# Two context weight pairs in one pass beside the first norm, and FFN token differences from whole normed values, made factor by factor

## The chip, the cores and the metric

One core of one Trainium2 chip runs the whole program. The metric is device microseconds from the first to the last instruction of one execution, as a median of several runs. TensorE (PE in the rows) multiplies, VectorE (DVE) and ScalarE (ACT) work on elements, GpSimd (POOL) takes some of the elementwise work, SyncE (SP) starts the transfers between main memory and the on-chip memory. Every engine takes its own instructions strictly in the order in which the built program lists them; semaphores hold an instruction until what it needs is there.

## The reference

One layer over 1024 latent tokens and 256 context tokens of width 1024, in fp32. What the change touches is this:

```python
hc = modulate(rms_norm(ctx, norm1_gain[layer]), csh1, csc1)
feats_c, post_c = mixer_inputs(hc, w_in[layer], ...)      # keys and values of the context, two mixers of 4 heads
hx = modulate(rms_norm(x, norm1_gain[layer]), sh1, sc1)   # first norm of the 1024 tokens
...
x = x + g1 * mixer_output(...)                            # ends in the product with w_out
x = x + g2 * swiglu(modulate(rms_norm(x, norm2_gain[layer]), sh2, sc2), w_ffn_in[layer], w_ffn_out[layer])
```

`modulate(h, shift, scale)` is `h * (1 + scale) + shift`, and `swiglu` is `(silu(gate) * up) @ w_ffn_out` with 2816 hidden channels.

## The kernel before

Features lie on the 128 partitions and tokens along the free axis, in two halves of 512 tokens. Each fp32 operand of a product is held as two parts: `split` (L190 to L192) writes the high part with a ScalarE cast (L191) and the low part with a VectorE subtraction (L192), and a product is three matmuls, high by high, high by low and low by high. A weight tile of 128x512 is loaded by SyncE into one of four tiles named `raw`, and split into one of seven tiles named `fw`. A scheduler places the instructions of all engines in an order that it works out when the program is built; the order of the Python lines is its priority.

**Context and first norm (L439 to L545).** The context's keys and values need four weight pairs, (pair, kt) with eight tiles of 128 features each; `ctx_tiles(pair, kts)` (L453) issues six matmuls for a tile, `ctx_load` (L445) loads and splits the next tile in the order of `ctx_order`. Pairs 0 and 1 run together while the modulation vectors are made. Then, in L530 to L534, each tile of pair 2 stands beside `scaled_x(0, kt)`, which multiplies a tile of the first token half by its root mean square (L484, VectorE), scales and shifts it twice on ScalarE (L402 for the high part, L404 for the whole value) and subtracts (L407, VectorE). Pair 3 follows in L536 to L541 after the sums of squares of the second half, with the loads of the first projection's weights (`plain_pair`) among it. Behind it come the gate products (L638) and the first keys, values, queries and gates (L265, in L644 to L656).

**Out-projection, second norm and the FFN's first blocks (L1131 to L1280).** For each token half, the out-projection gives `xf[hf]`, eight tiles, and two tiles `acc` of summed squares. `norm_steps` (L1142) then multiplies by the root mean square (L1152, VectorE) and calls `modulate_split` (L400): high part on ScalarE (L402), the whole value on GpSimd (L406, in place in `xf`), low part on VectorE (L407). `px0`, which holds `xf[0]`, is closed after the norm (L1183), so of the first half only the two parts remain, named `A` in the rows.

The FFN makes its first gate block and first up block in plain form, `plain_half` (L267), once for each token half. From the second block on it uses a seven-product form (`winograd_block`, L276), which needs differences of the token tiles: x11 and x21 are the upper and lower feature halves of the first tokens, x12 and x22 those of the second tokens. `right_factors(k)` (L1207) makes them for one k, with the first half put together again from its two parts:

```python
        tt(d, x22, x12, ALU.subtract)
        split(t3[0][k], t3[1][k], d)
        tt(x12, x12, b11[0][k].bitcast(F32), ALU.subtract)
        tt(x12, x12, b11[1][k].bitcast(F32), ALU.subtract)
        split(t1[0][k], t1[1][k], x12)
```

and so on to `t2` and to the value whose split in L1269 is `t4`. The weights of a seven-product block come from `Factors.make` (L234): s1 = a21 + a22 and s2 = s1 - a11 on VectorE, a11 - a21 on GpSimd, a12 - s2 on VectorE (all L237), each split. A block gives TensorE seven products of twelve matmuls in the tiles `ch` and `ts`; between them ScalarE copies the running `ch` tile into a tile `u` (L299), and TensorE may add the next product to `ch` only then. `run_blocks` puts the next block's first product after the fifth of the present one.

**The hidden tiles.** Of the plain blocks, ScalarE copies the result (L1255), and GpSimd multiplies up by the silu of gate (`up_done`, L1201). The four results of the first block are kept in `held_back`, and SyncE stores them (L1236) ahead of later loads. In SyncE's queue they stand before four loads of `cp` tiles for the kernel's last stage (L1378), and before the `raw` tiles of the second seven-product block.

## Time and profile before

| | us |
|---|---|
| median of 3 runs (1636.03, 1641.23, 5503.55) | 1641.23 |
| the profiled execution, its own time | 1639.88 |
| its span, first to last instruction | 1638.1 |
| TensorE busy in the span | 1571.9 (96%) |
| VectorE busy | 999.9 (61%) |
| ScalarE busy | 740.6 (45%) |
| GpSimd busy | 427.2 (26%) |
| mean granted TensorE clock, of full speed | 0.989 |

TensorE is busy nearly throughout, so a change that leaves the matmuls as they are can only move the rest: stretches in which TensorE stands still, and stretches after them in which its matmuls start further apart. In the waits view a row names who waited and which instruction released it. In the timeline a row is one or several like instructions with their start and duration, and behind them in brackets the idle time before and its releaser. Matmuls overlap, so the spacing of their starts is what one costs.

### The profile page before, as it was taken

The page shows a single profiled execution, that of the slowest core. Times are in us where ns is not written, and L with a number is a line of the kernel's source. Part 1 is how long each engine was busy: PE and PEld are TensorE (multiplying, and loading weights), DVE is VectorE, ACT ScalarE, POOL GpSimd, SP SyncE. Part 2 cuts the span into 40 slices and gives each one's busy share as a digit, 9 for nine tenths or more (in the row PEclk, how much of TensorE's full clock was granted, in tenths as well). Part 3 has the DMA queues.
Part 4 walks back from the last instruction along what each step waited for, and adds up shares of the span by engine and source line. Part 5 has one row for each costly group of instructions (what it writes and reads, how often), then busy time and mean ns, then how long its engine had stood idle before and what let it go on. Part 6 is the DMA issues. An engine that isn't in the chain of part 4 may idle for free.

```text
span 1638.1 us, 22335 instructions
## 1 busy us (share of the span) xinstructions
PE 1571.9 (96%) x7478; PEld 1282.6 (78%) x7478; DVE 999.9 (61%) x1843; ACT 740.6 (45%) x1430; POOL 427.2 (26%) x444
## 2 busy tenths in 40 slices
PE   7999979899999999999999998999999999999997
PEld 2678767778888777888888876888888888887887
DVE  4677787657657777766445786555555555546343
ACT  4676544444544575665223453334433334533230
POOL 0003225443335445420220254222222221001001
PEclk9999989999999999999999999999999999999998
DMA  8753547666666666647456413223222324835531
GB/s 293 265 156 105 154 141 241 193 197 198 185 180 222 200 207 206 189 143 263 142 167 198 130 45 103 78 84 96 91 90 77 95 86 148 271 102 181 167 96 52
DMA packets 178291, 255.47 MB, mean 156 GB/s; under 512 B 18128, under 2 KB 75984, under 8 KB 178176
## 3 DMA queue, kind: packets, MB, share of 16 engines
q1 hardware_dynamic: 176304, 251.95, 49.3%
q10 hardware_dynamic: 1872, 2.10, 0.4%
q8 instruction: 59, 0.97, 0.2%
q14 instruction: 56, 0.46, 0.1%
HBM read 197.60 MB, written 56.38 MB: 155 GB/s over the span
## 4 chain that ended last, share of the span: by engine, by line
PE 63%; DVE 8%; DMA 6%; issue 4%; ACT 3%; POOL 3%; SPq 0%; DVEq 0%; POOLq 0%; ACTq 0%
PE ch L265 20%; PE ts L265 15%; PE ch L1345 2%; PE ch L1344 2%; PE ch L1343 2%; PE ts L1343 2%; PE ts L1345 2%; PE ts L1344 2%; DMA stg<-wada 2%; PE ch L113 1%; PE ts L113 1%; PE ch L111 1%; PE ts L112 1%; PE ch L112 1%; PE ts L111 1%
## 5 line engine op out<-in xcount | busy, mean ns | idle before, releaser
L192 DVE TENSOR_TENSOR fw<-raw,fw 128x512 fp32r<-128x512 f32 x304 | 225.0, 745 | 145.9 <-ACT fw L191 145.1
L191 ACT CAST fw<-raw 128x512 fp32r<-128x512 f32 x304 | 187.0, 620 | 262.4 <-PE ts L265 88.6
L265 PE MATMUL ts<-A,fw 128*128 128x512 f32 x1200 | 295.3, 394 | 0.6 <-DVE kt L294 0.6
L265 PE MATMUL ch<-A,fw 128*128 128x512 f32 x1152 | 282.1, 393 | 9.6 <-ACT wt L299 9.6
L265 PE MATMUL ch<-t,fw 128*128 128x512 f32 x1008 | 254.2, 400 | 7.1 <-ACT u L299 5.5
L265 PEld LDWEIGHTS ts<-A,fw 128*128 128x128 f32 x1200 | 222.4, 188 | 46.4 <-DVE kt L294 1.6
L265 PEld LDWEIGHTS ch<-A,fw 128*128 128x128 f32 x1152 | 214.9, 188 | 55.2 <-ACT wt L299 10.2
L265 PEld LDWEIGHTS ch<-t,fw 128*128 128x128 f32 x1008 | 189.9, 191 | 47.4 <-ACT u L299 6.8
L1201 POOL TENSOR_TENSOR hid<-hid,sg 128x512 f32<-128x512 f32 x44 | 95.5, 2182 | 214.9 <-DVE hid L294 202.4
L299 ACT COPY u<-ch 128x512 f32<-128x512 f32 x104 | 60.8, 585 | 147.9 <-PE ch L265 147.8
L265 PE MATMUL ts<-t,fw 128*128 128x512 f32 x504 | 126.8, 399 | 0.0
L192 DVE TENSOR_TENSOR fw<-stg,fw 128x512 fp32r<-128x512 f32 x126 | 95.2, 755 | 40.2 <-ACT fw L191 39.9
L265 PEld LDWEIGHTS ts<-t,fw 128*128 128x128 f32 x504 | 95.4, 192 | 19.3
L237 POOL TENSOR_TENSOR stg<-raw,raw 128x512 f32<-128x512 f32 x42 | 65.1, 1549 | 160.7 <-DVE fw L192 86.2
L191 ACT CAST fw<-stg 128x512 fp32r<-128x512 f32 x126 | 78.5, 623 | 61.3 <-DVE stg L237 26.1
L868 POOL TENSOR_SCALAR vs<-kv,dcol 128x128 f32<-128x128 f32 x72 | 54.7, 770 | 54.6 <-PE sc L882 37.6
L591 POOL TENSOR_TENSOR wt<-wt,rp 128x512 f32<-128x512 f32 x16 | 28.8, 1800 | 152.4 <-ACT wt L590 140.4
L868 POOL TENSOR_SCALAR vs<-kv,colq 128x129 f32<-128x129 f32 x72 | 53.0, 745 | 54.4 <-PE sc L882 40.5
L1335 POOL TENSOR_SCALAR cp<-cp,cpack 128x256 f32<-128x256 f32 (+1 forms) x6 | 8.4, 1402 | 220.2 <-ACT stg L1389 220.2
L192 DVE TENSOR_TENSOR fw<-s,fw 128x512 fp32r<-128x512 f32 x42 | 30.6, 728 | 53.6 <-ACT fw L191 53.6
L1011 DVE SCALAR_TENSOR_TENSOR acc<-stg,silu_c,acc 128x512 f32<-128x512 f32 x56 | 47.7, 852 | 21.0 <-DMA stg<-wada 20.9
L882 PE MATMUL sc<-vs,kv 128*128 128x128 f32 (+1 forms) x288 | 47.5, 281 | 11.8 <-DVE wt L979 4.9
(374 smaller groups left out, 2939.4 us busy)
## 6 DMA issues: line engine op xcount, KB each, us to landing
raw<-wffn SPq DMA_DIRECT2D x88, 256.0 KB
raw<-wfo SPq DMA_DIRECT2D x88, 256.0 KB
raw<-win SPq DMA_DIRECT2D x64, 256.0 KB
stg<-wada SPq DMA_DIRECT2D x64, 256.0 KB
hid_d<-hid SPq DMA_DIRECT2D x44, 256.0 KB
kv<-kv_d SPq DMA_DIRECT2D x80, 128.0 KB
hraw<-hid_d SPq DMA_DIRECT2D x40, 256.0 KB
araw<-wada SPq DMA_DIRECT2D x32, 256.0 KB
```

What stands on the lines that cost most here:

```text
L191: nc.scalar.copy(hi, x)
L192: nc.vector.tensor_tensor(out=lo, in0=x, in1=hi.bitcast(F32), op=ALU.subtract)
L237: eng.tensor_tensor(out=o, in0=x, in1=y, op=op)
L265: nc.tensor.matmul(ps, lhsT=w[wp_][:, c], rhs=x[xp][k], start=start and k == i == 0, stop=cont or (stop and k == 3 and i == 2), skip_group ...
L299: nc.scalar.copy(o, chain)
L868: nc.gpsimd.tensor_scalar(out=vs, in0=kv[n][1], scalar1=col, scalar2=None, op0=ALU.mult)
L882: nc.tensor.matmul(ps, lhsT=kv[n][0], rhs=vsd.pop((d, n)), start=True, stop=True)
L1011: nc.vector.scalar_tensor_tensor(out=acc, in0=raw, scalar=s, in1=acc, op0=ALU.mult, op1=ALU.add)
L1201: nc.gpsimd.tensor_tensor(out=c, in0=c, in1=sgs[f, hf], op=ALU.mult)
L1343: nc.tensor.matmul(ps, lhsT=w[0][:, c], rhs=h[0][:, t], start=kt == 0, stop=False)
L1344: nc.tensor.matmul(ps, lhsT=w[0][:, c], rhs=h[1][:, t], start=False, stop=False)
L1345: nc.tensor.matmul(ps, lhsT=w[1][:, c], rhs=h[0][:, t], start=False, stop=kt == 2 * NG - 1)
```

## The change

The change has two parts and adds no arithmetic to the products. In the context stage, pair 3 is taken together with pair 2: `ctx_order` alternates the two, `ctx_tiles` of both stand beside `scaled_x(0, kt)`, and the first two `plain_pair` loads move in between. In the second norm and the FFN, `px0` moves to the left stack and stays open, so that `xf[0]` keeps the whole normed values of the first half; the summed squares use free `t` tiles; the whole value of the second half is made by ScalarE (L404) and no more by GpSimd; and `right_factors` makes one factor for all four k before the next, with the differences taken from `xf[0]`. It thus needs four VectorE subtractions or additions for a k where there were six, besides the three splits. The second up block's last weight tile uses two tiles of tag `u3` in place of `wx`.

```diff
--- before.py
+++ after.py
@@ -440,7 +440,7 @@
 
     ctx_ps, ctx_w = {}, {}
     ctx_order = ([(p, k) for k in range(6) for p in range(2)] + [(2, 0), (2, 1)] + [(p, k) for k in (6, 7) for p in range(2)]
-                 + [(2, k) for k in range(2, KT)] + [(3, k) for k in range(KT)])
+                 + [(3, 0), (3, 1)] + [(p, k) for k in range(2, KT) for p in (2, 3)])
 
     def ctx_load(n=1):
         for _ in range(n):
@@ -528,17 +528,14 @@
     cols_of("x0", x_raw[0], 512)
     load_x(x_raw[1], a["xT"][1])
     for kt in range(KT):
-        if kt >= 2:
-            ctx_tiles(2, (kt,))
-            ctx_load()
+        for pair in (2, 3):
+            if pair == 3 or kt >= 2:
+                ctx_tiles(pair, (kt,))
+                ctx_load()
         scaled_x(0, kt)
+        if kt in (4, 5):
+            plain_pair(w_kv, a["win"][0], kt - 4)
     cols_of("x1", x_raw[1], 512)
-    for kt in range(4):
-        ctx_tiles(3, (kt,))
-        ctx_load()
-    plain_pair(w_kv, a["win"][0], 0)
-    plain_pair(w_kv, a["win"][0], 1)
-    ctx_tiles(3, range(4, KT))
     plain_pair(w_qg, a["win"][1], 0)
     plain_pair(w_qg, a["win"][1], 1, last=tuple(st.tile([P, 512], F32R, tag="ss", bufs=2, name=nm("wl")) for _ in range(2)))
 
@@ -1134,7 +1131,7 @@
     hid_d = dram.tile([2 * NG, 2, P, 512], F32, name="hid_d")
     es_x1, es_x0 = ExitStack(), ExitStack()
     px1 = pool(es_x1, "px1")
-    px0 = pool(es_x0, "px0", side="right")
+    px0 = pool(es_x0, "px0")
     xf = [px0.tile([P, KT, 512], F32, name="xf0"), px1.tile([P, KT, 512], F32, name="xf1")]
 
     hh = []
@@ -1150,14 +1147,14 @@
         for kt in range(KT):
             xr = xf[hf][:, kt, :]
             nc.vector.tensor_tensor(out=xr, in0=y, in1=xr, op=ALU.mult)
-            modulate_split(xr, h2[0][:, kt, :], h2[1][:, kt, :], a2[:, kt:kt + 1], mod2[:, 8 + kt:9 + kt], xr)
+            modulate_split(xr, h2[0][:, kt, :], h2[1][:, kt, :], a2[:, kt:kt + 1], mod2[:, 8 + kt:9 + kt], xr, hf == 1)
             if kt % 2:
                 yield
 
     norm = iter(())
     out_w = ahead([a["wout"][i, kh] for _ in range(2) for i in range(4) for kh in range(2)])
     for hf in range(2):
-        acc = [px0.tile([P, 512], F32, tag="acc", bufs=4, name=nm("acc")) for _ in range(2)]
+        acc = [t_tile(1, hf, k, F32) for k in range(2)]
         for i in range(4):
             w = next(out_w) + next(out_w)
             for mt in range(2):
@@ -1180,7 +1177,6 @@
         norm = norm_steps(hf, acc)
     for _ in norm:
         pass
-    es_x0.close()
 
 
     pe = pool(es, "pe", side="right")
@@ -1204,23 +1200,24 @@
         else:
             nc.sync.dma_start(hid_d[2 * gidx + f, hf], c)
 
-    def right_factors(k):
-
-        x12, x22 = xf[1][:, k, :], xf[1][:, 4 + k, :]
+    def right_factors():
 
         def tt(o, x, y, op):
             nc.vector.tensor_tensor(out=o, in0=x, in1=y, op=op)
 
-        d = tmp("cp")
-        tt(d, x22, x12, ALU.subtract)
-        split(t3[0][k], t3[1][k], d)
-        tt(x12, x12, b11[0][k].bitcast(F32), ALU.subtract)
-        tt(x12, x12, b11[1][k].bitcast(F32), ALU.subtract)
-        split(t1[0][k], t1[1][k], x12)
-        tt(x22, x22, x12, ALU.subtract)
-        split(t2[0][k], t2[1][k], x22)
-        tt(x22, b21[0][k].bitcast(F32), x22, ALU.subtract)
-        tt(x22, x22, b21[1][k].bitcast(F32), ALU.add)
+        (x11, x21), (x12, x22) = ([[xf[hf][:, 4 * i + k, :] for k in range(4)] for i in range(2)] for hf in range(2))
+        d = [tmp("cp") for _ in range(4)]
+        for k in range(4):
+            tt(d[k], x12[k], x11[k], ALU.subtract)
+            split(t1[0][k], t1[1][k], d[k])
+        for k in range(4):
+            tt(x12[k], x22[k], x12[k], ALU.subtract)
+            tt(x22[k], x12[k], x11[k], ALU.add)
+            split(t2[0][k], t2[1][k], x22[k])
+        for k in range(4):
+            split(t3[0][k], t3[1][k], x12[k])
+        for k in range(4):
+            tt(x22[k], x21[k], x22[k], ALU.subtract)
 
     sgs = {}
     def ffn_blocks():
@@ -1246,8 +1243,7 @@
                 yield block(g, part, sgs)
 
     w0 = plain_quads(a["wffn"][0, 0])
-    wx = pe.tile([P, 2, 512], F32R, name="wx")
-    w1 = plain_quads(a["wffn"][0, 1], (wx[:, 0, :], wx[:, 1, :]))
+    w1 = plain_quads(a["wffn"][0, 1], tuple(pe.tile([P, 512], F32R, tag="u3", bufs=2, name=nm("wx")) for _ in range(2)))
 
     def plain_copy(tag, done):
         def fn(ps, f, hf):
@@ -1260,14 +1256,14 @@
     up_copy = plain_copy("hid", lambda f, hf, c: up_done(0, sgs, f, hf, c))
     plain_half(w0, b_all, 0, gate_copy)
     plain_half(w1, b_all, 0, up_copy)
-    for k in range(4):
-        right_factors(k)
+    right_factors()
     seven_blocks = list(ffn_blocks())
     plain_half(w0, b_all, 1, gate_copy)
     seven_blocks[0][0].load()
     plain_half(w1, b_all, 1, up_copy)
     for k in range(4):
         split(t4[0][k], t4[1][k], xf[1][:, 4 + k, :])
+    es_x0.close()
     es_x1.close()
     ph0 = pool(es, "ph0", side="right")
     early = [tuple(ph0.tile([P, 512], F32R, tag=f"e{s}", bufs=4, name=nm("eh")) for s in range(2)) for _ in range(4)]
```

The scheduler turns this into another order. **ScalarE's queue beside the first norm, before** (`fw<-raw` is the high part of a weight tile, `A` and `t` the high part and the whole value of a token tile):

```order
L191 CAST fw178_724<-raw177_722 128x512
L402 ACTIVATE A1_116<-stg175_706,sh1_81,a1_82 128x512
L404 ACTIVATE t5_120<-stg175_706,sh1_81,a1_82 128x512
L402 ACTIVATE A1_116<-stg176_711,sh1_81,a1_82 128x512
L404 ACTIVATE t6_121<-stg176_711,sh1_81,a1_82 128x512
L402 ACTIVATE A1_116<-stg179_727,sh1_81,a1_82 128x512
L404 ACTIVATE t7_122<-stg179_727,sh1_81,a1_82 128x512
L191 CAST fw181_740<-raw180_738 128x512
L402 ACTIVATE A1_116<-stg182_743,sh1_81,a1_82 128x512
L404 ACTIVATE t8_123<-stg182_743,sh1_81,a1_82 128x512
```

and now:

```order
L191 CAST fw177_714<-raw176_712 128x512
L402 ACTIVATE A1_116<-stg179_719,sh1_81,a1_82 128x512
L404 ACTIVATE t5_120<-stg179_719,sh1_81,a1_82 128x512
L191 CAST fw181_732<-raw180_730 128x512
L402 ACTIVATE A1_116<-stg182_735,sh1_81,a1_82 128x512
L404 ACTIVATE t6_121<-stg182_735,sh1_81,a1_82 128x512
L191 CAST fw184_748<-raw183_746 128x512
L191 CAST fw186_759<-raw185_757 128x512
L402 ACTIVATE A1_116<-stg187_762,sh1_81,a1_82 128x512
L404 ACTIVATE t7_122<-stg187_762,sh1_81,a1_82 128x512
L191 CAST fw189_775<-raw188_773 128x512
L191 CAST fw191_786<-raw190_784 128x512
```

One cast stood among three tiles of the norm at first and then one for each; now there are two for each token tile from the third on.

**VectorE's queue from the end of the second norm on, before** (`cp` are the differences, `t` the low parts of the factors, `A2271` and `A2272` the parts of the first token half, `xf0` and `xf1` the two halves, `A2311` and `A2312` the second half's parts):

```order
L407 TENSOR_TENSOR A2312_9661<-xf1_8923,A2311_9660 128x512 x4
L1212 TENSOR_TENSOR cp2360_9874<-xf1_8923 128x512
L1212 TENSOR_TENSOR cp2361_9887<-xf1_8923 128x512
L1212 TENSOR_TENSOR xf1_8923<-xf1_8923,A2271_9365 128x512
L192 TENSOR_TENSOR t2333_9718<-cp2360_9874,t2329_9714 128x512
L1212 TENSOR_TENSOR xf1_8923<-xf1_8923,A2272_9366 128x512
L192 TENSOR_TENSOR t2334_9719<-cp2361_9887,t2330_9715 128x512
L1212 TENSOR_TENSOR xf1_8923<-xf1_8923 128x512
L192 TENSOR_TENSOR t2317_9702<-xf1_8923,t2313_9698 128x512
L1212 TENSOR_TENSOR xf1_8923<-xf1_8923,A2271_9365 128x512
L192 TENSOR_TENSOR t2325_9710<-xf1_8923,t2321_9706 128x512
L1212 TENSOR_TENSOR xf1_8923<-xf1_8923,A2272_9366 128x512
```

and now:

```order
L407 TENSOR_TENSOR A2312_9661<-xf1_8923,A2311_9660 128x512 x2
L1206 TENSOR_TENSOR cp2362_9874<-xf1_8923,xf0_8922 128x512
L1206 TENSOR_TENSOR cp2363_9875<-xf1_8923,xf0_8922 128x512
L407 TENSOR_TENSOR A2312_9661<-xf1_8923,A2311_9660 128x512 x2
L1206 TENSOR_TENSOR cp2364_9876<-xf1_8923,xf0_8922 128x512
L1206 TENSOR_TENSOR cp2365_9877<-xf1_8923,xf0_8922 128x512
L1206 TENSOR_TENSOR xf1_8923<-xf1_8923 128x512
L407 TENSOR_TENSOR A2312_9661<-xf1_8923,A2311_9660 128x512 x2
L1206 TENSOR_TENSOR xf1_8923<-xf1_8923,xf0_8922 128x512
L1206 TENSOR_TENSOR xf1_8923<-xf1_8923 128x512 x2
L192 TENSOR_TENSOR t2317_9701<-cp2362_9874,t2313_9697 128x512
L192 TENSOR_TENSOR t2318_9702<-cp2363_9875,t2314_9698 128x512
```

The first four differences now stand inside the norm, taken from `xf` of both halves, and the rest follows in runs of one kind.

**SyncE's queue around the four stores of hidden tiles, before** (`raw2397` to `raw2400` are the four weight tiles of the second seven-product block, `raw2399` to `raw2402` after the change):

```order
L211 DMA raw2397_10110<-wffn 128x512
L1236 DMA hid_d_8915<-hid2357_9843 128x512
L1236 DMA hid_d_8915<-hid2359_9871 128x512
L1378 DMA cp2939_13240<-x1_d_8914 128x512
L1378 DMA cp2940_13242<-x1_d_8914 128x512
L1378 DMA cp2941_13244<-x1_d_8914 128x512
L1378 DMA cp2942_13246<-x1_d_8914 128x512
L211 DMA raw2398_10112<-wffn 128x512
L1236 DMA hid_d_8915<-hid2373_10015 128x512
L211 DMA raw2399_10114<-wffn 128x512
L1236 DMA hid_d_8915<-hid2375_10043 128x512
L211 DMA raw2400_10116<-wffn 128x512
```

and now:

```order
L211 DMA raw2399_10103<-wffn 128x512
L1233 DMA hid_d_8915<-hid2359_9843 128x512
L1374 DMA cp2941_13233<-x1_d_8914 128x512
L1374 DMA cp2942_13235<-x1_d_8914 128x512
L1233 DMA hid_d_8915<-hid2361_9871 128x512
L1374 DMA cp2943_13237<-x1_d_8914 128x512
L1374 DMA cp2944_13239<-x1_d_8914 128x512
L211 DMA raw2400_10105<-wffn 128x512
L211 DMA raw2401_10107<-wffn 128x512
L1233 DMA hid_d_8915<-hid2375_10007 128x512
L211 DMA raw2402_10109<-wffn 128x512
L211 DMA raw2424_10249<-wffn 128x512
```

The second store now stands behind two of the `cp` loads; two weight loads follow before the third store, where one did.

## Rows read from the trace of the kernel before

**Rows 1.** What TensorE waited for over the whole span: us in total, times, longest
```profile
PE ch L265 <- ACT wt L299: 9.6, 1, 9.6
...
PE ch L265 <- ACT u L299: 5.5, 3, 3.4
...
PE ts L462 <- ACT fw L191: 2.0, 3, 0.9
```

**Rows 2.** Timeline of TensorE, context pairs: start us, us, instruction, [idle before <- releaser]
```profile
64.71 0.40 PE L462 MATMUL ts<-fw,t 128*128 128x512 f32 x1
...
70.28 1.84 PE L150 MATMUL sc<-ones,ss 128*128 128x1 f32 x16
71.98 0.48 PE L462 MATMUL sc<-fw,t 128*128 128x512 f32 x1
...
81.26 0.40 PE L462 MATMUL ts<-fw,t 128*128 128x512 f32 x1
...
99.42 0.40 PE L265 MATMUL ts<-A,fw 128*128 128x512 f32 x1
```

**Rows 3.** Timeline of ScalarE: a weight cast, then scaling and shift of the first norm
```profile
59.55 0.62 ACT L191 CAST fw<-raw 128x512 fp32r<-128x512 f32 x1 [0.18 <-PE ch L464]
...
78.49 0.81 ACT L402 ACTIVATE A<-stg,sh,a 128x512 fp32r<-128x512 f32 x1 [0.52 <-DVE stg L484]
79.21 0.81 ACT L404 ACTIVATE t<-stg,sh,a 128x512 f32<-128x512 f32 x1
```

**Rows 4.** Timeline of ScalarE: a cast that waits for its weight load
```profile
105.69 0.62 ACT L191 CAST fw<-raw 128x512 fp32r<-128x512 f32 x1 [3.33 <-DMA raw<-win]
```

**Rows 5.** Timeline of SyncE's queue, the load that rows 4 wait for
```profile
103.01 1.35 SPq L436 DMA_DIRECT2D raw<-win  x3
```

**Rows 6.** Timeline of TensorE, first block of the FFN's seven-product form
```profile
988.23 2.89 PE L265 MATMUL ch<-A,fw 128*128 128x512 f32 x12
990.96 2.88 PE L265 MATMUL ts<-t,fw 128*128 128x512 f32 x12
995.66 4.60 PE L265 MATMUL ch<-t,fw 128*128 128x512 f32 x12 [1.82 <-ACT u L299]
...
1006.37 4.61 PE L265 MATMUL ch<-t,fw 128*128 128x512 f32 x12 [3.37 <-ACT u L299]
1010.82 2.43 PE L265 MATMUL ch<-A,fw 128*128 128x512 f32 x10
```

**Rows 7.** Timeline of ScalarE, the cast ahead of the copy that TensorE last waits for
```profile
1005.22 0.62 ACT L191 CAST fw<-stg 128x512 fp32r<-128x512 f32 x1 [9.09 <-DVE stg L237]
```

**Rows 8.** Timeline of VectorE, second norm's end, the differences' end, next block's sum
```profile
964.48 1.77 DVE L407 TENSOR_TENSOR A<-xf,A 128x512 fp32r<-128x512 f32 x1 [0.59 <-POOL xf L406]
...
992.67 0.68 DVE L192 TENSOR_TENSOR fw<-stg,fw 128x512 fp32r<-128x512 f32 x1
993.28 0.68 DVE L237 TENSOR_TENSOR stg<-raw,s 128x512 f32<-128x512 f32 x1
994.64 1.00 DVE L192 TENSOR_TENSOR fw<-stg,fw 128x512 fp32r<-128x512 f32 x1 [0.69 <-ACT fw L191]
...
1004.44 0.69 DVE L237 TENSOR_TENSOR stg<-raw,raw 128x512 f32<-128x512 f32 x1 [7.10 <-DMA raw<-wffn]
```

**Rows 9.** Timeline of SyncE's queue, stores of hidden tiles and loads behind them
```profile
965.74 29.70 SPq L1236 DMA_DIRECT2D hid_d<-hid  x2
...
997.45 0.38 SPq L211 DMA_DIRECT2D raw<-wffn  x1
...
998.41 0.37 SPq L211 DMA_DIRECT2D raw<-wffn  x1
```

**Rows 10.** Timeline of GpSimd, first product of hidden tiles
```profile
964.42 1.29 POOL L1201 TENSOR_TENSOR hid<-hid,sg 128x512 f32<-128x512 f32 x1
```

**Rows 11.** The same, second product
```profile
971.69 23.39 POOL L1201 TENSOR_TENSOR hid<-hid,sg 128x512 f32<-128x512 f32 x1 [5.98 <-ACT hid L1255]
```

**Rows 12.** What VectorE waited for from 925 to 1015 us
```profile
DVE A L407 <- POOL xf L406: 4.6, 7, 1.2
```

## The prediction

> **What bounds the kernel now.** I read TensorE's list of waits first [rows 1]. Three entries matter. The longest, 9.6 us, lies at the mixers' gates; the change leaves that stage's order as it was. The other two lie where the change works: 2.0 us behind ScalarE's casts in the context stage and, in the second entry, 5.5 us behind ScalarE's copies `u`, nearly all of it in the FFN's first seven-product block. Then I read TensorE's timeline at both places, because idle time alone understates them: starts also drift apart around a wait.
>
> In the context stage, 24 matmuls of pairs 0 and 1 start between 64.71 and 70.28, so one costs 0.232 us [rows 2]. The 16 small matmuls of the squares' sums cost 71.98 - 70.28 = 1.70 us. From 81.26 to 99.42 there are the 48 matmuls of pair 3 and another such 16. They should take 48 x 0.232 + 1.70 = 12.84 us and take 18.16, so 5.3 us are lost. The cause is ScalarE: beside the norm, one token tile needs two activations that start 0.72 us apart and a cast of 0.62 [rows 3], 2.06 us, while pair 2 alone gives TensorE 6 x 0.232 = 1.39 us of work. TensorE runs through pair 2 early and then gets pair 3's tiles one by one, between the norm's activations.
>
> In the FFN, a product of twelve matmuls takes 990.96 - 988.23 = 2.73 us [rows 6]. Five products stand from 988.23 to 1010.82, and should take 13.6 of these 22.6 us: 9.0 us are lost, in two waits and in two products that take 4.60 and 4.61 us instead of 2.88. The last wait is read backwards. ScalarE's copy stood behind a cast that had waited 9.09 us for VectorE's sum [rows 7]; the sum had waited 7.10 us for a weight load [rows 8]; SyncE issued that load only at 998.41, because its two stores of hidden tiles held the queue from 965.74 on for 29.70 us [rows 9]; and the second store waited for GpSimd's product, which took 23.39 us [rows 11] where the first took 1.29 [rows 10]. GpSimd started it at 971.69 and ended with the first pause of VectorE, 0.69 us ahead of 994.64 [rows 8]. So VectorE's unbroken string of subtractions both delays its own later work and shuts GpSimd out, and through the store it shuts out the next weights. The first wait, 1.82 us, is the same backlog: the string's last pass ahead of that cast, `stg<-raw,s`, begins only at 993.28.
>
> **Part one, pairs 2 and 3 together.** Now a token tile of the norm brings TensorE 12 x 0.232 = 2.78 us of matmuls, ScalarE 2 x 0.72 + 2 x 0.62 = 2.68 us, and VectorE four passes of 0.61 [rows 8], 2.44 us. TensorE is the longest of the three by a little, so it should hardly wait, and its rows of 81 to 99 close up. No instruction is added. Behind the pairs the first projection starts on token tiles whose last one comes just then: ScalarE's eight pairs of activations now carry fourteen casts among them, and this last tile and the second root mean square may each hold TensorE for some tenths of a microsecond. No row shows that wait. It is bounded by 0 and by two activations, 1.4 us; I take 0.5, nearer to 0, since TensorE still has another output tile's products to do. Loads come twice as fast, from four `raw` tiles. A load issued at 103.01 was there for a cast at 105.69, 2.7 us [rows 4, 5]; with a cast and a pass of together 1.3 us a tile is in use for 4.0 us, so four give one per 1.0 us, where TensorE needs one per 1.39. Earlier in the stage casts wait for TensorE to free a tile, not for a load [rows 3]. Term: -5.3 + 0.5 = -4.8 us. Its bounds are -5.3 and 0.
>
> **Part two, the norm on ScalarE.** Eight GpSimd instructions go, eight activations of 0.72 us come: 16 x 0.72 = 11.5 us for the whole second half, while TensorE runs the first half's plain products. VectorE's 4.6 us of waits for GpSimd inside the norm go [rows 12], and differences fill part of its pauses. The norm's last VectorE pass stays near 964; TensorE reads the last tile several microseconds later. So nothing on the path, and if this cover failed, each microsecond that the norm ends later would be one of TensorE's.
>
> **Part three, the differences.** Before, 9 VectorE passes for each of four k, four for `t4` and six for weights stand between the norm's last pass at 964.48 and 993.28: 46 passes, 28.8 us. Now a k has 7 passes, so 28 are left; 5 of them stand ahead of the norm's last pass, the four of `t4` and one weight pass go behind. That leaves 28 passes, 28 x 0.61 = 17 us, so `stg<-raw,s` starts at about 981 and no more at 993. The first wait's cast then comes some 7 us before its copy is due, and the 1.82 us and the first stretched product go.
>
> For the second wait, GpSimd counts. ScalarE's copies come after the sixteen activations, so even the first product of hidden tiles meets an unbroken string. I assume that it ends only at VectorE's next pause, about 982.5, 12 us earlier than before. Before, the two `raw` loads went out 2.4 and 3.3 us after the pause's end at 994.64 plus the product; now one more product, one more store and two more `cp` loads lie on that way, so I put the loads at 986. Taken at the slow figure of the row, 1004.44 - 998.41 = 6.0 us, they land at 992; the sum that stood at 1004.44 stands there, and the copy due at 996.4 is not held. What is late next is the fourth `raw` tile. It can only be loaded after seven more passes, 992 + 4.3 = 996.5, lands 2.7 to 6.0 us later, and two passes after it, at 1000.4 to 1003.7, the next block's first weight is whole. TensorE wants it after five products, 988.23 + 13.6 = 1001.8. The wait is 0 to 1.9 us; I take 0.6. Term: -9.0 + 0.6 = -8.4 us, bounds -9.0 and 0.
>
> The Trainium skill's page "SBUF — State Buffer" ("SBUF: two separate sides") says that VectorE with two SBUF inputs and GpSimd take a shared pair of ports as an exclusive lock, held for a whole instruction, and that the loser blocks fully. Rows 10 and 11 agree, 1.29 against 23.39 us. The rule speaks against part two: with ScalarE feeding it, VectorE pauses less, and the product that had slipped in at 964.42 is locked out too. By it the forecast above stands only if the string is as short as counted; without the lock the loads would be out by about 982, and the 0.6 us would be 0.
>
> **The rest.** The loads of the first half's x tiles move behind two weight loads, and a wait for TensorE stands before the first. TensorE's list has no entry there; I take 0, and at most the one load's 2.7 us. The moved sums and the `wx` tile cost nothing on any engine.
>
> **Sum.** 1639.88 - 4.8 - 8.4 = 1626.7 us, against the profiled execution's own time. That execution lies 1.35 us below the median shown, so the gain is 13.2 us against the one and 14.5 us, 0.9%, against the other. About 2% is what a measurement of this kernel can tell from no change.
>
> **Rivals.** First, only the FFN's part comes through: in the context stage the wait moves to the norm's last tile or into the gates' wait of 9.6 us, whose releaser is a chain of other engines [rows 1]. For it speaks that ScalarE is within 4% of TensorE's load; against it, that this chain is started by TensorE's own progress. Time 1639.88 - 8.4 = 1631.5.
>
> Second, only the context part: the lockout outlasts my count. If the string ended as late as before, the loads would be no earlier and all 9.0 us would stay: 1639.88 - 4.8 = 1635.1. Each microsecond that the loads go out after about 985 costs one, so half of the loss is there at 990. The count of passes is against it.
>
> Third, slower: the supply of weight tiles in the context stage. With a landing time L, a tile comes every (L + 1.3) / 4 us, and the sixteen from pair 2's fifth to the first projection's fourth are held up once this passes 1.39, at L = 4.3. At 6.0, which the FFN's load took [rows 8, 9], they lose 16 x 0.43 = 6.9 us, more than the 5.3 gained. Above L = 7.7 they eat up both gains; at 9 they cost 16 x 1.19 = 19 us: 1639.88 + 19 - 5.3 - 8.4 = 1645.2. Against it: 2.7 us in the same stage.
>
> Fourth, the change does not do what it says: TensorE's waits stay, because the order around them is the same. The order shown contradicts that. Time 1640.
>
> **How the numbers follow.** Forecast 66%, first rival 15%, second 13%, slower 4%, no effect 2%. The first two rivals lie at 1631.5 and 1635.1, so a range up to 1636 takes them in, and down to 1620 it takes in both terms at their full 5.3 and 9.0 with some microseconds for the spread of the runs, 1636.03 to 1641.23. None of the cases lies beyond 2% of the median on either side; I leave 1% for each.
>
> **What would show it.** In the changed kernel's profile TensorE's matmuls of the pairs should start 0.23 us apart up to the first projection; the first five products of the seven-product form should take under 15.5 us; VectorE's `stg<-raw,s` should start near 981 and GpSimd's first product of hidden tiles should be the long one, over 15 us. SyncE's two `raw` loads should go out about 986. I am wrong if TensorE's list still has the casts of the context stage with more than 1.5 us, if the copies `u` still hold it for over 2 us, or if the gates' wait has grown by what the context stage gained.

## The result, and the profile of the changed kernel

The changed kernel takes 1631.8 us in the median of 14 runs, the kernel before 1638.4 us beside it. The ratio is 0.9943 with a 95% interval of 0.9931 to 0.9956, so some 9 us, or 0.6%, are gained. A second measurement gave 0.9950 (0.9933 to 0.9968). Forecast were 1626.7 us and a gain of 13.2 us, 0.8%. The range of 1620 to 1636 holds the result, and it lies within 2% as forecast, but about 4 us of the gain are missing. Ratios are turned into microseconds below with 1640 us. The profiled execution took 1634.83 us, its span 1633.0 us; it was the slowest of the 14.

**The context stage did what was forecast.** The first fence is TensorE's busy time in the stretch where the kernel before lost 5.3 us [rows 2], of the kernel before; the columns are the stretch, its length, TensorE's busy time (matmuls), the granted clock, the share of the DMA engines and GB/s. The second is the same of the changed kernel.

```profile
81.30:99.40 18.10, 15.17 (x65) 1.00 0.57 167
```

```profile
81.30:99.40 18.10, 18.10 (x80) 1.00 0.76 241
```

TensorE issues 80 matmuls there where it had issued 65, and none of them waits.

**What came of this lead.** TensorE's timeline from the first transposes of the projections (`sc<-cpack,kt`) through the projections' first seven-product block, from its second product, `ts<-t`, to its sixth, `ch<-A`; first the kernel before, then the changed one.

```profile
127.86 0.60 PE L579 MATMUL sc<-cpack,kt 128*128 128x128 f32 x4
...
158.03 3.01 PE L265 MATMUL ts<-t,fw 128*128 128x512 f32 x12
161.39 2.56 PE L265 MATMUL ch<-t,fw 128*128 128x512 f32 x10 [0.35 <-ACT u L299]
165.55 0.73 PE L265 MATMUL ch<-t,fw 128*128 128x512 f32 x2 [1.60 <-DVE t L192]
166.13 2.89 PE L265 MATMUL ts<-A,fw 128*128 128x512 f32 x12
168.86 2.88 PE L265 MATMUL ch<-t,fw 128*128 128x512 f32 x12
171.58 2.89 PE L265 MATMUL ch<-A,fw 128*128 128x512 f32 x12
```

```profile
122.74 0.60 PE L576 MATMUL sc<-cpack,kt 128*128 128x128 f32 x4
...
152.90 3.01 PE L265 MATMUL ts<-t,fw 128*128 128x512 f32 x12
157.50 2.35 PE L265 MATMUL ch<-t,fw 128*128 128x512 f32 x9 [1.59 <-ACT u L299]
161.17 0.50 PE L265 MATMUL ch<-t,fw 128*128 128x512 f32 x1 [1.32 <-ACT t L191]
162.33 0.72 PE L265 MATMUL ch<-t,fw 128*128 128x512 f32 x2 [0.66 <-DVE t L192]
162.89 4.51 PE L265 MATMUL ts<-A,fw 128*128 128x512 f32 x12
167.24 2.91 PE L265 MATMUL ch<-t,fw 128*128 128x512 f32 x12
169.99 2.89 PE L265 MATMUL ch<-A,fw 128*128 128x512 f32 x12
```

At the transposes the changed kernel is 127.86 - 122.74 = 5.1 us ahead, at the sixth product only 171.58 - 169.99 = 1.6. The block took 13.55 us from its second to its sixth product (four products, 4 x 2.73 = 10.9 us without a wait) and now takes 17.09. Two things make up most of the 3.5 us: the waits grew from 1.95 to 3.57 us, and the product behind them took 4.51 us in place of 2.89. VectorE, which makes the differences of x for this block (`t`), did not come 5.1 us earlier. Its first sum of the next weights, before and after, and from before also the low parts that TensorE waits for last:

```profile
146.76 0.69 DVE L237 TENSOR_TENSOR stg<-raw,raw 128x512 f32<-128x512 f32 x1 [2.92 <-DMA raw<-win]
...
164.81 1.29 DVE L192 TENSOR_TENSOR t<-wt,t 128x512 fp32r<-128x512 f32 x2
```

```profile
142.92 0.69 DVE L237 TENSOR_TENSOR stg<-raw,raw 128x512 f32<-128x512 f32 x1 [2.98 <-DMA raw<-win]
```

That is 3.8 us earlier. From there on VectorE has no pause until the block's last factors are made, and the low parts of 164.81 start at 161.59 (shown with the experiments below), 3.2 us earlier. So much of the lead TensorE still had at the product behind the waits (162.89 against 166.13), and the longer product took 1.6 of it.

**The FFN's seam.** The FFN's first plain product in the kernel before, then TensorE's timeline of the changed kernel from that product on, which answers to [rows 6]:

```profile
941.81 3.33 PE L265 MATMUL ts<-A,fw 128*128 128x512 f32 x14
```

```profile
944.27 3.33 PE L265 MATMUL ts<-A,fw 128*128 128x512 f32 x14
949.05 1.05 PE L150 MATMUL sc<-ones,t 128*128 128x1 f32 x8 [1.45 <-DVE t L1141]
...
991.87 2.89 PE L265 MATMUL ch<-A,fw 128*128 128x512 f32 x12
994.60 2.88 PE L265 MATMUL ts<-t,fw 128*128 128x512 f32 x12
997.32 2.88 PE L265 MATMUL ch<-t,fw 128*128 128x512 f32 x12
...
1005.48 2.88 PE L265 MATMUL ch<-A,fw 128*128 128x512 f32 x12
```

Five products take 1005.48 - 991.87 = 13.6 us: all of the 9.0 us that were lost there are gone. VectorE, GpSimd and SyncE's queue in the changed kernel, for [rows 8 to 11]:

```profile
941.61 0.69 DVE L192 TENSOR_TENSOR wx<-raw,wx 128x512 fp32r<-128x512 f32 x1 [3.21 <-ACT wx L191]
942.21 0.74 DVE L1168 SCALAR_TENSOR_TENSOR xf<-ts,mod,xf 128x512 f32<-128x512 f32 x1
...
974.11 3.42 DVE L192 TENSOR_TENSOR t<-xf,t 128x512 fp32r<-128x512 f32 x2
...
985.88 0.68 DVE L237 TENSOR_TENSOR stg<-raw,s 128x512 f32<-128x512 f32 x1
...
989.40 0.89 DVE L237 TENSOR_TENSOR stg<-raw,raw 128x512 f32<-128x512 f32 x1 [2.23 <-DMA raw<-wffn]
```

```profile
967.62 9.36 POOL L1197 TENSOR_TENSOR hid<-hid,sg 128x512 f32<-128x512 f32 x2 [17.50 <-ACT hid L1251]
987.20 1.29 POOL L1197 TENSOR_TENSOR hid<-hid,sg 128x512 f32<-128x512 f32 x1 [10.22 <-ACT hid L1251]
```

```profile
975.31 0.33 SPq L1233 DMA_DIRECT2D hid_d<-hid  x1
...
977.01 0.32 SPq L1233 DMA_DIRECT2D hid_d<-hid  x1
...
984.22 2.74 SPq L211 DMA_DIRECT2D raw<-wffn  x2
...
990.36 4.99 SPq L211 DMA_DIRECT2D raw<-wffn  x2
```

The stores no longer hold the queue, and the sum that had stood 16 us behind the block's first product (1004.44 against 988.23) stands 2.5 us ahead of it. But there is a new wait, 1.45 us at the second norm's sum of squares (L150). Its chain begins with the first of VectorE's rows: the split of `wx` waits 3.21 us, and behind it stand the last residual tiles `xf`, of which the squares are summed. From the plain products' start to the block's first product it was 988.23 - 941.81 = 46.4 us, now 47.6.

**The gates' wait is what it was** [rows 1]; of the copies `u` no entry is over 1.6 us:

```profile
PE ch L265 <- ACT wt L299: 9.6, 1, 9.6
...
PE ch L265 <- ACT u L299: 1.6, 1, 1.6
```

### The profile page after: what moved, and what is told of

It reads as the page before. It is cut to its first block, busy times and chain, and to the rows that moved or that the text cites. A ratio compares the mean times of both kernels' runs of the same rounds, so it can differ in the third digit from the quotient of the medians.

```text
span 1633.0 us, 22343 instructions
## 1 busy us (share of the span) xinstructions
PE 1570.3 (96%) x7478; PEld 1284.6 (79%) x7478; DVE 995.4 (61%) x1835; ACT 745.7 (46%) x1438; POOL 404.1 (25%) x436
## 3 DMA queue, kind: packets, MB, share of 16 engines
q1 hardware_dynamic: 176304, 251.95, 48.7%
## 5 line engine op out<-in xcount | busy, mean ns | idle before, releaser
L265 PEld LDWEIGHTS ch<-A,fw 128*128 128x128 f32 x1152 | 215.3, 189 | 55.2 <-ACT wt L299 10.2
L265 PE MATMUL ch<-t,fw 128*128 128x512 f32 x1008 | 250.2, 395 | 3.6 <-ACT u L299 1.6
L1197 POOL TENSOR_TENSOR hid<-hid,sg 128x512 f32<-128x512 f32 x44 | 79.8, 1824 | 235.8 <-DVE hid L294 176.2
```

The source lines that it names most:

```text
L265: nc.tensor.matmul(ps, lhsT=w[wp_][:, c], rhs=x[xp][k], start=start and k == i == 0, stop=cont or (stop and k == 3 and i == 2), skip_group ...
L1197: nc.gpsimd.tensor_tensor(out=c, in0=c, in1=sgs[f, hf], op=ALU.mult)
```

## The experiments

The theory: the lead of 5.1 us is spent at the block of 152 to 170, because the second factor's last two tiles stand in VectorE's queue behind the third and fourth factors of the tiles before, and TensorE's clock falls behind that wait; and 1.2 us are lost at the squares' sum. Against it stood: the context part passes its gain on and the FFN part falls short; or the scans between 204 and 944 us take it away.

**The two parts alone.** `ctx_only` is the kernel before with

```diff
-                 + [(2, k) for k in range(2, KT)] + [(3, k) for k in range(KT)])
+                 + [(3, 0), (3, 1)] + [(p, k) for k in range(2, KT) for p in (2, 3)])
...
+        for pair in (2, 3):
+            if pair == 3 or kt >= 2:
+                ctx_tiles(pair, (kt,))
+                ctx_load()
...
```

and `ffn_only` is the changed kernel with these lines, and the moved `plain_pair(w_kv, ...)`, as before.

> The kernel before with the context part of the change alone (third and fourth pairs tile by tile, loads as in the change). Theory A, given back: TensorE reaches the first transposes behind w_qg some 5 us earlier, but the differences of x that the first seven-product block reads come only 3.8 us earlier, TensorE waits longer for them (3.6 us of waits between 152 and 168 instead of 1.95) and the granted clock falls to half behind these waits; 1.6 us of lead are left at the block's second half, so the time falls by 1.6 us (0 to 3). Theory B, passed on in full: 4.8 us less, and what the changed kernel lacks of its 13.2 us is lost in the FFN part. Theory C, lost in the scans between 204 and 944 us: the lead is 4 to 5 us at 190 and gone at 900.

> The kernel before with the part behind the scans alone (whole normed values, differences factor by factor, the second norm's whole values on ScalarE, the tiles' new places); the context stage as before. Theory A: 9.0 us of waits and half clock go from the first seven-product block, 1.2 us come in at the second norm's sum of squares: 7.8 us less (6.5 to 9). Theory B, which has the missing 4 us in this part: 4.5 us less. The first block's five products take 13.6 us without a wait by both.

Measured: `ctx_only` 0.9999 (0.9985 to 1.0014), nothing; `ffn_only` 0.9966 (0.9955 to 0.9977), 5.6 us. In `ctx_only` the block at 152 us took 17.09 us, as in the changed kernel; in `ffn_only` 13.72. In `ffn_only` the FFN's five products took 13.61 us, and 47.75 us lie from the plain products to the block, as in the changed kernel. So the context part alone gives nothing where 4.8 us were forecast, and theory B, full passing on, falls for it; the traces place its loss at the block. The times do not place all that is missing. `ffn_only` gained less than the 7.8 us that its two seams show: 7.8 lies just outside its interval (3.8 to 7.4), the 4.5 us of theory B inside it, and where the rest went is open. The two parts alone add up to 5.8 us, which the intervals do not tell from the 9.3 of the whole change.

**Two choices within the FFN part.** `norm_pool` puts the second norm's whole values back on GpSimd; `per_k` makes the same differences tile by tile.

```diff
-            modulate_split(..., xr, hf == 1)
+            modulate_split(..., xr)
```

```diff
-        for k in range(4):
-            tt(d[k], x12[k], x11[k], ALU.subtract)
-            split(t1[0][k], t1[1][k], d[k])
-        for k in range(4):
+        for k in range(4):
+            d = tmp("cp")
+            tt(d, x12[k], x11[k], ALU.subtract)
+            split(t1[0][k], t1[1][k], d)
             tt(x12[k], x22[k], x12[k], ALU.subtract)
+            split(t3[0][k], t3[1][k], x12[k])
             tt(x22[k], x12[k], x11[k], ALU.add)
             split(t2[0][k], t2[1][k], x22[k])
-        for k in range(4):
-            split(t3[0][k], t3[1][k], x12[k])
-        for k in range(4):
             tt(x22[k], x21[k], x22[k], ALU.subtract)
```

> The changed kernel with one part undone: the second norm's eight whole values are made on GpSimd again, from the scaled tile as before, and ScalarE makes the rounded values alone. If the prediction's part two is right (nothing on the path, TensorE reads the tiles later): the same time as the changed kernel, within 1.5 us. Rival: GpSimd's passes are stretched while VectorE works, the low parts and the differences behind them come late, and the first seven-product block waits again: 3 to 9 us slower than the changed kernel, with stg<-raw,s near 990.

> The changed kernel with the differences made k by k (all of one k's factors, then the next) from the same whole values with the same 28 passes, in place of factor by factor. If the count of passes carries the gain: the same time as the changed kernel, within 1.5 us. Rival, the order carries it: the differences of the first products come later, the second block half waits for the last k or the block's weight sums move: 2 to 5 us slower.

Measured: 0.9955 (0.9938 to 0.9971) and 0.9959 (0.9943 to 0.9976), both the changed kernel's gain within the intervals, and in both the five products take 13.61 us. So neither the engine of the norm nor the order of the differences carries the gain; what both keep is the 28 passes. That their number carries it follows by exclusion: no run varied it alone. `norm_pool` shows GpSimd's lockout once more:

```profile
964.39 1.29 POOL L1197 TENSOR_TENSOR hid<-hid,sg 128x512 f32<-128x512 f32 x1
972.27 16.85 POOL L1197 TENSOR_TENSOR hid<-hid,sg 128x512 f32<-128x512 f32 x2 [6.59 <-ACT hid L1251]
```

The first product slips in before the string, as in [rows 10]; the next two take 16.85 us until 989.1. The Trainium skill's page "SBUF — State Buffer" ("SBUF: two separate sides") has GpSimd blocked for as long as VectorE's two-input passes hold the shared ports; these rows agree with it, 1.29 us free against 16.85 for two. And yet TensorE waits for nothing here, so the lockout alone does not cost time.

**The order of the differences in the projections.** `x_by_factor` does for the block at 152 us what the change does in the FFN. The passes are the same; the second factor's tiles go ahead of most of the third's and fourth's (second 0, 1; last 0, second 2; last 1, second 3; last 2, 3).

```diff
-    def other_factors(k):
+    def second_factor(k):
+        d3s[k], d2s[k] = wt(), wt()
+        nc.vector.tensor_tensor(out=d3s[k], in0=x22, in1=x12, op=ALU.subtract)
+        nc.vector.tensor_tensor(out=d2s[k], in0=d3s[k], in1=x11, op=ALU.add)
+        put_factor(t2, d2s[k], (1, 0, k), (3, 0, k))
+    def last_factors(k):
+        nc.vector.tensor_tensor(out=d2s[k], in0=x_raw[0][4 + k], in1=d2s[k], op=ALU.subtract)
+        put_factor(t3, d3s[k], (3, 1, k), (1, 1, k))
+        split(t4[0][k], t4[1][k], d2s[k])
...
-                    other_factors(2 * key + f)
+                    for step, k in (((0, 0), (0, 1)), ((1, 0), (0, 2)), ((1, 1), (0, 3)), ((1, 2), (1, 3)))[2 * key + f]:
+                        (second_factor, last_factors)[step](k)
```

`late_wx` holds the split of `wx` back until the squares are summed up, and `x_by_factor_late_wx` does both.

```diff
+    wx = tuple(pe.tile([P, 512], F32R, tag="u3", bufs=2, name=nm("wx")) for _ in range(2))
+    nc.vector.tensor_copy(wx[0][:, 0:1], acc[0][:, 0:1])
+    w1 = plain_quads(a["wffn"][0, 1], wx)
```

`after_again` is the changed kernel itself, beside these three on the same chip.

> The changed kernel as it is, a second profile and its time on the chip that the next three run on. By its first 14 runs: 0.9943 of the kernel before. In the profile, if the losses behind the context stage belong to the change and not to one run: the same three waits of 3.6 us in all between 152 and 163, granted clock 0.83 in 160 to 170, 1.2 to 1.6 us of wait at the second norm's sum of squares, five products of the first FFN block in 13.6 us.

> The changed kernel with the differences of x for the projections' first seven-product block made by factor, as the change does it in the FFN: the second factor's four before most of the third's and fourth's, with the same 32 VectorE passes. Theory A (the lead of the context stage is lost because the second factor's last two tiles stand behind the third and fourth factors of the tiles before, and the clock falls behind that wait): the waits between 152 and 163 shrink from 3.6 to under 2 us, the clock stays at 1.00 in 160 to 170, the lead of 5 us reaches 170, and the time falls by 2 to 4 us against the changed kernel. Theory B (VectorE has too little time there whatever the order): the wait moves to a later product of the block and the time stays within 1 us. Theory C (what is won there is lost in the scans): the lead at 170 is 5 us and the time is the same.

> The changed kernel with the split of the FFN's last plain weight quarter (wx) held back until the second norm's sum of squares is summed up, as it stood before the change, by one copy of a single column. If the wait of 1.45 us at the sum of squares comes from this split, which waits for its load ahead of the last residual tiles on VectorE: the wait goes, 1.2 us less. Rival: VectorE's tiles are late anyway or the load behind the held weight tile comes late: no change, or up to 2 us more at the first FFN block.

> Both edits of the two kernels before in one: if the losses are separate, their gains add up (3 to 5 us against the changed kernel, 13 against the kernel before, which is the prediction's whole sum).

Measured:

| kernel | ratio to before | 95% interval | block at 152 us, second to sixth product | plain FFN start to the FFN's first block |
|---|---|---|---|---|
| `after_again` | 0.9950 | 0.9933 to 0.9968 | 17.00 us | 46.9 us |
| `x_by_factor` | 0.9911 | 0.9895 to 0.9928 | 11.01 us | 48.7 us |
| `late_wx` | 0.9934 | 0.9918 to 0.9950 | 15.51 us | 46.2 us |
| `x_by_factor_late_wx` | 0.9904 | 0.9886 to 0.9923 | 10.99 us | 46.1 us |

`after_again` showed the rows expected of it, but for a wait of only 0.78 us at the squares' sum. Theory A holds. TensorE's timeline in `x_by_factor` has no wait in the block, and the block is 6 us shorter than in the changed kernel, which is about what the time gained (0.9950 - 0.9911, 6.4 us, by the two intervals some 4 either way). That is more than the 2 to 4 us expected: besides the 3.5 us by which the block had grown, 2.5 us went that it had lost in the kernel before (13.55 to 11.01).

```profile
151.88 3.01 PE L265 MATMUL ts<-t,fw 128*128 128x512 f32 x12
...
162.89 2.88 PE L265 MATMUL ch<-A,fw 128*128 128x512 f32 x12
```

VectorE's queue shows the cause. The low parts that TensorE waits for at the end of its second factor come at 161.59 in the changed kernel, behind passes for the rotation, the weights and the last factors; in `x_by_factor` they come at 149.73. First the changed kernel, then `x_by_factor`:

```profile
156.87 0.69 DVE L593 SCALAR_TENSOR_TENSOR kt<-kt,rp 128x512 f32<-128x512 f32 x1
157.48 1.78 DVE L671 TENSOR_TENSOR wt<-t,t 128x512 f32<-128x512 f32 x1
...
161.59 1.28 DVE L192 TENSOR_TENSOR t<-wt,t 128x512 fp32r<-128x512 f32 x2
```

```profile
149.73 1.28 DVE L192 TENSOR_TENSOR t<-wt,t 128x512 fp32r<-128x512 f32 x2
```

`late_wx` happens to measure the clock by itself. Its waits in the block add up to 3.64 us, as many as the changed kernel's 3.57, but in its profile the clock stayed up. TensorE from 150 to 170 us in the changed kernel, and in `late_wx` (columns as above):

```profile
150.00:160.00 10.00, 8.26 (x37) 1.00 0.31 102
160.00:170.00 10.00, 8.17 (x28) 0.83 0.22 65
```

```profile
150.00:160.00 10.00, 8.35 (x41) 1.00 0.35 110
160.00:170.00 10.00, 8.00 (x35) 1.00 0.23 66
```

The block took 17.09 - 15.51 = 1.6 us less. For the squares' sum `late_wx` shows what was expected in the profile: the wait is gone and the stretch before the FFN's block is 46.2 us, as before the change. In time it gained 2.6 us on `after_again`, which the intervals do not tell from none. `x_by_factor_late_wx` shows both gains in its profile; its time is 15.7 us (12.6 to 18.7) under the kernel before, where 13 was expected, and only 1.1 us under `x_by_factor`, which the intervals do not tell from none either.

**What the context part is worth once it is covered.** `x_by_factor_no_ctx` is `x_by_factor` with the context part taken back, `x_by_factor_again` the kernel with both beside it.

```diff
-                 + [(3, 0), (3, 1)] + [(p, k) for k in range(2, KT) for p in (2, 3)])
+                 + [(2, k) for k in range(2, KT)] + [(3, k) for k in range(KT)])
```

> The kernel with the differences of x made by factor once more, to stand beside the next on the same chip: 0.991 of the kernel before (0.9895 to 0.993).

> The same kernel with the context part of the change undone (third pair, then fourth, as before): what the context part is worth when the first seven-product block waits for nothing. If the prediction's term of 4.8 us was right and only its cover was missing: 4 to 5 us slower than the kernel with both (0.994 of the kernel before), 5 us behind it at the fifth product of the first block, at the gates and at the end. Rival, the gates' wait or the scans take the lead away anyway: within 1.5 us of the kernel with both.

Measured: 0.9916 (0.9897 to 0.9935) with the context part, 0.9946 (0.9931 to 0.9961) without; the medians are 1628.94 and 1634.24 us, 5.3 us apart. Without the context part the block takes as long as with it:

```profile
158.85 2.99 PE L265 MATMUL ts<-t,fw 128*128 128x512 f32 x12
...
169.84 2.43 PE L265 MATMUL ch<-A,fw 128*128 128x512 f32 x10
```

10.99 us, from a start 158.85 - 153.66 = 5.2 us later than in `x_by_factor_again`. So with the old order of x's differences the context part is worth 0.2 us on the kernel before, or 3 on the FFN part, and with the new order about 5, by the two intervals some 4 either way. The gates' wait does not take it away: it is 10.2 us without the context part, and 10.2 to 11.1 in the three profiles with it. Of the scans the profiles say less. From the gates' transposes to the FFN it is 713 us without it and 709, 711 and 716 with it, and in all kernels with unchanged lines there it is between 708.6 (the kernel before) and 716.1, with no order by the context part. So one profile of that stretch can neither show nor exclude a loss of some microseconds, and the times have to decide.

**A version beyond both.** In all these kernels TensorE waits 10 us at the gates for a copy on ScalarE (`wt<-ch`). ScalarE's timeline of the changed kernel shows that it stands behind the copies for the rotation, and these behind VectorE:

```profile
220.44 0.62 ACT L586 COPY wt<-kt 64x512 f32<-64x512 f32 x1 [2.96 <-DVE kt L294]
...
221.71 0.59 ACT L299 COPY wt<-ch 128x512 f32<-128x512 f32 x1
```

`rotate_later` adds to `x_by_factor_late_wx`

```diff
-                    later(1, rotate, c, hf, QSCALE if part else None)
-                later(2 if ret else 1, store, qk_d[u][:, 1 - part, t], c)
+                    later(2, rotate, c, hf, QSCALE if part else None)
+                later(3 if ret else 1, store, qk_d[u][:, 1 - part, t], c)
```

and puts the transposes behind it (`later(4 ...` to `later(5 ...`).

> Both edits (differences of x by factor, the split of wx held back) and, besides, the rotation of each head's tiles one product later in the program, with its store and transpose: ScalarE's copy of the running product, for which TensorE waits 9.6 to 10.2 us at the gates, then stands ahead of the copies that wait for VectorE's gate scans. If that wait is set by ScalarE's order alone: it shrinks to about 6 us, and 3 to 5 us go from the time of the kernel with both edits (0.9904 of the kernel before). Rival: TensorE waits for VectorE's sums there a product later, or the scans start later: no gain, or up to 5 us more.

Measured: 0.9840 (0.9822 to 0.9858), 26 us under the kernel before and 10 under `x_by_factor_late_wx`, twice what was expected. TensorE's list of waits, and its busy time from 250 to 400 us, in `rotate_later`:

```profile
PE ch L265 <- ACT wt L299: 4.2, 1, 4.2
...
PE sc L576 <- DVE kt L294: 3.3, 2, 2.5
```

```profile
250.00:400.00 150.00, 144.22 (x787) 0.99 0.72 218
```

and that busy time in `x_by_factor_late_wx`:

```profile
250.00:400.00 150.00, 138.97 (x722) 0.94 0.66 203
```

The wait of 10.2 us shrank to 4.2, and another of 2.5 took part of its place. From the first transposes to the gates' own it is 102.3 us against 103.5, so little of the 10 us comes from there; the stretch behind it is busier by 5.2 us, at a clock of 0.99 in place of 0.94. In the profiles of `x_by_factor` and `x_by_factor_again` it is busy for 138.22 and 139.12 us at 0.98 and 0.97, so the 5 us hold against all three, and most of the difference in the clock does not. Why that stretch fills up was not tried further.

## Why the prediction was right or wrong

**Part one: the loss of 5.3 us was right, its cover was not.** TensorE runs without a wait from 81.3 to 99.4 us, and leads by 5.1 us at the transposes. The step that failed is the one that ended the term at -4.8: it looked for a new wait at the norm's last tile and the second root mean square, put it at 0.5, and took the rest as passed on to the end. The new wait lay 50 us further on, at the first block that reads differences of x. There a wait of 1.95 us already stood in the trace of before, which the prediction did not read: TensorE was waiting for VectorE's queue, and it could keep only as much of a lead as that queue came earlier, 3.2 of the 5.1 us; 1.6 of these went with the clock behind the waits. None of the signs of being wrong appeared, since they watched the casts, the copies `u` and the gates, and not this block. The term measured 5.1 - 3.5 = 1.6 us by the traces, 0.2 in `ctx_only` with an interval of 2.5 either way. The first rival had such a wait, at the gates or the norm's last tile, and 1631.5 us; its time is the one measured, its places are not, for the gates' wait stayed at 9.6. With VectorE's queue put in order, the term is near the 4.8 forecast (5.2 by the traces at the block, 5.3 between the medians).

**The third rival**, a shortage of weight tiles in the context stage, did not come: no wait, at 241 GB/s in that stretch.

**Part two, nothing on the path**, was right; `norm_pool` shows that GpSimd does as well. Its forecast that the first product of hidden tiles is locked out too was right, its length was not: the first took 7.66 us in the changed kernel and both together 9.36, not over 15. Nor did they have to wait for VectorE's next pause: from 967.42 to 987.2 VectorE had none. They came through inside its string, where two of its passes (974.11) took 3.42 us in place of 1.3.

**Part three, -9.0 in full.** The count of 28 passes and the earlier `stg<-raw,s` hold: it stands 6.0 us ahead of the block's first product, forecast 7. The 0.6 us for a late fourth tile did not occur: its load went out at 990.36, 1.5 us ahead of the block's first product (991.87), where the forecast had it 8.3 behind (996.5 against 988.23). There are two reasons. The two loads before it went out 7.7 and 5.2 us ahead of that product (984.22 and 986.63), where the forecast had 2.2 for both. And the sum that waited for the second of them started 989.40 - 986.63 = 2.8 us after that load went out, where 6.0 was taken. `norm_pool` tests the second rival's price as well: its loads went out from 988.31 on, 0.4 us ahead of the block, a point at which the rival had 2.9 us of loss; there was none. The landing was the mis-sized number again: the sum started at 992.94, 3.3 us after the second load went out at 989.68.

**The rest, "the `wx` tile costs nothing",** was wrong. Its new place frees its split early enough to stand in VectorE's queue ahead of the residual tiles, where it waits for its load. The stretch it lies in is 0.5 to 2.3 us longer in the eight profiles with the early split (46.9 to 48.7 us) than the 46.4 of before, and 46.1 to 46.2 in the three with the split held back.

Added up by the two traces at the places that the change touches: -5.1 + 3.5 - 9.0 + 1.2 = -9.4 us, against a measured 9.3 (7.2 to 11.3). That the two agree so well is in part luck, for the two profiled executions are only 1639.88 - 1634.83 = 5.1 us apart. In these two, the changed kernel loses another 4.1 us between the block at 152 us and the FFN: 1.6 us ahead at the sixth product, it is 2.5 us behind at the first plain product (944.27 against 941.81). Most of it lies in the stretch behind the gates, whose length differs by as much among profiles of kernels with the same lines there. Whether any of it belongs to the change is open.

## What to carry to other kernels

A lead is worth what the next shared queue lets through: after a stall is removed, follow the lead down the trace to the next place where the engine already waits, however short that wait is, and ask whether its releaser comes earlier too. Where products read differences tile by tile, make the tiles of the factor that is read first ahead of those of the next where the reader waits for them: this order was worth 6 us in the projections, where TensorE waited for VectorE, and nothing in the FFN, where it did not (`per_k`). And a tile that moves to memory that is free earlier also moves its split forward in an in-order queue, ahead of work that is more urgent.

## What the runs showed of the hardware

TensorE's clock made a short wait cost nearly half as much again. Behind 3.6 us of waits between 152 and 163 us it was granted 0.83 of the full clock from 160 to 170 in five of the six profiles that had those waits (in the changed kernel 0.50, the 1.2 GHz level, from 164 to 166), and 1.00, the 2.4 GHz level, in the sixth (`late_wx`); the difference was 1.6 us. With waits of 1.95 and 2.10 us there, the kernel before and `ffn_only` kept 1.00. In the kernel before, the stretches from 990 to 1000 and from 1000 to 1010 have 0.83 each, and of the 9.0 us lost there 3.4 are the two products of 4.60 and 4.61 us [rows 6] in place of 2.88; they went together with the waits.
